# A chunk's norm in three queued steps, six gate products on GpSimd, and two drains less before the retention scan

## Chip, cores and metric

One core of one Trainium2 chip. The metric is the device time of one launch in microseconds (us), the median of several runs of the kernel.

## What is computed

A stream of 512 latent tokens and 256 context tokens, D = 1024, passes two layers. Layer 0 has a bidirectional mLSTM mixer (8 heads, keys of 64, values of 128), layer 1 a bidirectional retention mixer (8 heads, keys and values of 128). After each mixer stands a mixture of 16 experts with expert choice. All is float32. Of the first mixer's scan, per head and direction:

```python
s = einsum('bhid,bhjd->bhij', qc, kc) * exp(dmat - m_row[..., None])
num = einsum('bhij,bhjv->bhiv', s, vc) + w_inter[..., None] * einsum('bhid,bhdv->bhiv', qc, C)
den = s.sum(-1) + w_inter * einsum('bhid,bhd->bhi', qc, n)
h = num / maximum(abs(den), exp(-m_row))[..., None]
C_new = wc[..., None, None] * C + einsum('bhj,bhjd,bhjv->bhdv', wk, kc, vc)
```

The two directions are added, each head's 128 values are normed by their root mean square, multiplied by the norm's gain and by the sigmoid of an output projection, and projected back. The retention mixer is the same without the normaliser, with a fixed decay per head.

## The kernel before

Projections run in three matmul passes: weights and activations are each split into a high and a low part (`whi`, `wlo`, `hT_hi`, `hT_lo`), and `mm3` (L312 to L314) adds hi x hi, hi x lo and lo x hi in one PSUM tile `acc`. A pass of `Proj.run` takes 512 columns: for each token tile and each of 8 slices `k` it issues one triple of matmuls on 128x512. `split_piece` makes the parts, `whi` on ScalarE (L318) and `wlo` on VectorE (L319).

Beside the passes run generators. `bg` is a list of them; after every triple, `bg.step()` moves each on by one part, and a yielded number delays it by so many steps. `bg.drain()` runs all to their end at once. This sets the order in which instructions are handed to a scheduler, which orders each engine's queue from there. `tc.issue_after` queues what stands in it behind a given instruction. Nearly all transfers are issued by SyncE's queue, in order.

The first mixer's scan is worked in two blocks of four heads. `scan0(blk)` (L670) goes over six chunks of 128 tokens. `load` fetches qk, V, the rows E and the weights qw; `load_states` fetches the states Cz; `prep` (L706) masks E by GpSimd's affine_select (L711), takes eight exponentials on ScalarE (L715) and multiplies qw on VectorE (L717); `scores` (L720) makes S by matmul (L725) and A = S x E on VectorE (L731), four of them; `outputs` (L733) makes the numerators `num` (L739 with the states, L742 with A), the denominators `dn` and their reciprocal `rd`, and `yo` (L755 on ScalarE for one direction, L757 on VectorE for the other). `normed` (L760) takes the square on ScalarE (L762), a sum on VectorE (L764), a scale (L765), the power -1/2 on GpSimd (L766), and a product on VectorE (L767). `states` (L605) makes the states of the next block: `kw` on GpSimd (L612), `cu` by matmul (L618), C on VectorE (L622, L624), written by SyncE to DRAM (L628) for `load_states`.

The output projection is the pass that runs beside block 1's states and scan and beside the rest of block 0. Its end of a tile is `o_done` (L633): sigmoid on ScalarE (L636), times the gain `ng` on GpSimd (L637), times the normed chunk on VectorE (L638), write to DRAM (L639). There are six tiles per block, twelve in all.

In the retention mixer, `done` turns each projected q and k tile by rope (`qr`, `Kt`, the last step on GpSimd, L1694); `spill_T` (L1701) transposes it on TensorE (`tT`, L1705) and writes it to DRAM. `scan(blk)` (L1767) builds decay tables, then takes four chunks: it loads q, k, V and two states, makes scores `Sp`, `Ar`, `qs` and outputs `ro` (L1817), and norms them. Block 1's scan runs beside the pass of the gate.

Of the kernel before, what the change touches and what calls it, by code (L numbers as in the profile page):

```python
# [9 lines left out]
F32 = mybir.dt.float32  # L10
# [4 lines left out]
OP = mybir.AluOpType  # L15
# [5 lines left out]
T_LAT = 512  # L21
# [24 lines left out]
def backbone(ctx, tc, x, c, ctx_in, c_ctx, ada_w, ada_b, norm_mix_g, norm_ffn_g, final_norm_g,  # L46
# [460 lines left out]
    def mlstm_mixer(R):  # L507
# [125 lines left out]
        def o_done(blk, ng):  # L633
            def f(tt, p):
                e = pc.tile([128, 512], F32, name="oe", bufs=2)
                nc.scalar.activation(e, p, AF.Sigmoid)  # L636
                nc.gpsimd.tensor_tensor(e, e, ng, op=OP.mult)  # L637
                nc.vector.tensor_tensor(e, e, Y[blk, tt].rearrange("p h v -> p (h v)"), op=OP.mult)  # L638
                nc.sync.dma_start(y_d[0][tt][:, blk * 512:(blk + 1) * 512], e)  # L639
                gated.append(tt)  # L640
            return f
# [28 lines left out]
    def scan0(blk, sb, sp, pc, cols, flo, Y, gated):  # L670
# [35 lines left out]
        def prep(cc):  # L706
            t = L[cc]
            for d in range(2):
# [7 lines left out]
                if cc in prev0[d]:  # L716
                    nc.vector.scalar_tensor_tensor(t["qw"][:, d], t["qk"][:, 0:2], 0.125, t["qw"][:, d],  # L717
                                                   op0=OP.mult, op1=OP.mult)

        def scores(cc):  # L720
# [6 lines left out]
            for d in range(2):  # L727
                A = t["A", d] = sb.tile([128, 2, 2, 128], F32, name=f"A{d}")
                Ev = t["E"][:, d].rearrange("p (g q) i -> p q g i", q=2)
                for q in range(2):  # L730
                    nc.vector.scalar_tensor_tensor(A[:, q], S[q], 0.125, Ev[:, q], op0=OP.mult, op1=OP.mult)  # L731

# [26 lines left out]

        def normed(cc, y):  # L760
            j = sb.tile([128, 4, 128], F32, name="ysq", bufs=1)
            nc.scalar.activation(j, y, AF.Square)  # L762
            ss, rs = st("yss"), st("yrs")
            nc.vector.tensor_reduce(ss[:, 0:4], j, axis=mybir.AxisListType.X, op=OP.add)  # L764
            nc.vector.tensor_scalar(ss[:, 0:4], ss[:, 0:4], 1.0 / 128, EPS, op0=OP.mult, op1=OP.add)  # L765
            nc.gpsimd.tensor_tensor(rs[:, 0:4], ss[:, 0:4], neghalf[:, 0:4], op=OP.pow)  # L766
            nc.vector.tensor_tensor(y, y, rs[:, 0:4, None].to_broadcast([128, 4, 128]), op=OP.mult)  # L767
        load(order0[0])
# [6 lines left out]
        scores(order0[0])  # L775
        yield 1
        for n, cc in enumerate(order0):
            if n + 2 < len(order0):
                load(order0[n + 2])
            if n + 1 < len(order0):  # L780
                prep(order0[n + 1])
                yield 3
                scores(order0[n + 1])
                yield 4
            while len(gated) < 6 * blk + n - 5:
                yield 1
            y = pc.tile([128, 4, 128], F32, name="yo", bufs=6)
            outputs(cc, 0, y)
            yield 1
            outputs(cc, 1, y)  # L790
            normed(cc, y)
            Y[blk, cc] = y
            if n + 2 < len(order0):
                load_states(order0[n + 2])
            yield 2

    def gates(P, pp, tt_, wgp, gb, cols, flo, wcb, colp):
# [866 lines left out]
    def retention_mixer(R):  # L1664
# [33 lines left out]
        def ada_sums():  # L1698
            return [tmp[0].tile([128, 1024], F32, name="adasum", tag=f"y{i}", bufs=1) for i in (1, 2)]

        def spill_T(src, dst, tt):  # L1701
            yield 6
# [4 lines left out]
            nc.scalar.activation(t, p, AF.Copy)  # L1707
            nc.sync.dma_start(dram_ap(dst, (tt - 2) * 128, [[T_LAT, 128], [128 * T_LAT, 4], [1, 128]]), t)

        def done(what, blk):  # L1710
# [56 lines left out]
        def scan(blk):  # L1767

            sb = tmp[0]
            qd = [sb.tile([128, 4, 128], F32, name=f"qd{d}", bufs=1) for d in range(2)]  # L1770
            Dm = sb.tile([128, 4, 128], F32, name="Dm", bufs=1)
# [20 lines left out]
            yield 1  # L1792
            for cc in order1:
                tsl = [[T_LAT, 128], [128 * T_LAT, 4], [1, 128]]
                q = sb.tile([128, 4, 128], F32, name="qT", bufs=1)
                nc.sync.dma_start(q, dram_ap(qT_d[blk], (cc - 2) * 128, tsl))
                k = sb.tile([128, 4, 128], F32, name="kT", bufs=1)
                nc.sync.dma_start(k, dram_ap(kT_d[blk], (cc - 2) * 128, tsl))
                V = sb.tile([128, 4, 128], F32, name="Vr", bufs=1)
                nc.sync.dma_start(V.rearrange("p a b -> p (a b)"), Vr_d[blk][(cc - 2) * 128:(cc - 1) * 128, :])  # L1800
                S = []
                for d in range(2):
                    S.append(sb.tile([128, 4, 128], F32, name=f"Sl{d}", bufs=1))
                    nc.sync.dma_start(S[d].rearrange("p a b -> p (a b)"), S_d[blk][d, cc - 2])
                p = pp.tile([128, 4, 128], F32, name="Sp", tag="b", bufs=2)
# [42 lines left out]
        P.run(0, order1, done("q", 0), nxt=1536)  # L1848
        bg.drain()
        bg.add(scan(0), 0)  # L1850
# [4 lines left out]
        P.run(512, order1, done("q", 1), nxt=3072)  # L1855
        bg.drain()
        bg.add(scan(1), 2)
# [108 lines left out]
```

## Time and profile before

| | |
|---|---|
| three runs, us | 1913.15, 1916.28, 1919.35 |
| median, us | 1916.28 |
| the profiled execution, us | 1921.03 |
| its span, us | 1919.2 |
| mean granted clock of TensorE | 0.982 |
| busy share of the span: TensorE, VectorE, ScalarE, GpSimd | 95%, 38%, 22%, 15% |

The span is the time from the first to the last instruction; 1.8 us of the profiled execution lie around it. Times in the rows are us from the span's start unless marked ns. PE is TensorE's matmuls, DVE is VectorE, ACT ScalarE, POOL GpSimd, SP SyncE. A row names the line of the kernel, the engine, the operation and out<-in by the program's names. In a timeline, what stands in brackets is how long the engine stood idle before and what ended it. PEclk is the share of its full clock that TensorE was granted. Matmuls overlap, so two starts that follow each other tell the pace better than one's duration. The stages: the first mixer's scan and output lie at 240 to 480 us, the first mixture of experts up to 1060, the retention mixer up to about 1360, and the second mixture of experts behind.

### The profile page before, as it was taken

How to read it: one execution, taken by the hardware profiler on the slowest of the kernel's cores; microseconds unless marked ns; L12 is line 12 of the kernel's file. 1: busy time of each engine (PE TensorE's matmuls, PEld its weight loads, DVE VectorE, ACT ScalarE, POOL GpSimd, SP SyncE). 2: the span in 40 equal slices, each digit the busy share in tenths (PEclk: the TensorE clock that was granted, in tenths of full speed). 3: DMA queues.
4: the chain of work that ended last, by engine and by line, in shares of the span. 5: the costliest groups of instructions: out<-in, count | busy, mean ns of one | idle time of the engine just before them, and what ended most of it. 6: DMA issues, size and time to landing. Idle time of an engine off the chain costs nothing. (4 is left out here: it accounts for less than half of the span.)

```text
span 1919.2 us, 27783 instructions
## 1 busy us (share of the span) xinstructions
PE 1814.5 (95%) x11093; PEld 1029.8 (54%) x11093; DVE 730.0 (38%) x1742; ACT 429.1 (22%) x839; POOL 285.3 (15%) x343
## 2 busy tenths in 40 slices
PE   6999988999899999999999999999979999999997
PEld 2765676788444434444444777788764333333332
DVE  3554557646311111111113678454571322222224
ACT  3623356342200000000003621332421010100001
POOL 1110124201121111111001224334200000000001
PEclk9999999999899999999999999999998999999999
DMA  8568777672899999999996588445738999999996
GB/s 273 209 210 273 261 190 206 197 270 84 303 368 391 383 388 398 377 401 379 407 412 234 194 291 274 130 153 188 285 154 306 421 421 420 421 421 421 421 420 247
DMA packets 168578, 585.42 MB, mean 305 GB/s; under 512 B 16674, under 2 KB 68578, under 8 KB 114690
## 3 DMA queue, kind: packets, MB, share of 16 engines
q1 hardware_dynamic: 160176, 570.72, 78.3%
q0 software_dynamic: 6912, 12.71, 3.1%
q8 instruction: 88, 1.44, 0.3%
q10 hardware_dynamic: 1362, 0.23, 0.1%
q14 instruction: 40, 0.33, 0.0%
HBM read 544.13 MB, written 39.47 MB: 304 GB/s over the span
## 5 line engine op out<-in xcount | busy, mean ns | idle before, releaser
L1327 PE MATMUL y<-wslot,hT 128*32 128x256 f32 (+1 forms) x2016 | 278.7, 488 | 8.6 <-ACT hT L1493 8.4
L1327 PE MATMUL gl<-wslot,xs 128*64 128x512 f32 x1024 | 236.2, 605 | 7.1 <-DMA wslot<-in_moe_w_gate_dram 6.1
L1327 PE MATMUL ul<-wslot,xs 128*64 128x512 f32 x1024 | 229.9, 595 | 1.9 <-DMA wslot<-in_moe_w_up_dram 1.9
L312 PE MATMUL acc<-whi,hT_hi 128*128 128x512 f32 x544 | 223.3, 412 | 4.4 <-ACT hT_hi L382 3.1
L313 PE MATMUL acc<-wlo,hT_hi 128*128 128x512 f32 x544 | 218.0, 401 | 0.0
L314 PE MATMUL acc<-whi,hT_lo 128*128 128x512 f32 x544 | 217.3, 399 | 0.2 <-DVE hT_lo L383 0.2
L1327 PEld LDWEIGHTS y<-wslot,hT 128*32 128x32 f32 (+1 forms) x2016 | 100.0, 123 | 171.4 <-issue 131.8
L1476 DVE TENSOR_TENSOR hid<-hid,ul 128x512 f32<-128x512 f32 x32 | 22.0, 688 | 372.5 <-PE ul L1327 372.5
L1327 PEld LDWEIGHTS gl<-wslot,xs 128*64 128x64 f32 x1024 | 71.8, 138 | 155.5 <-issue 134.3
L1327 PEld LDWEIGHTS ul<-wslot,xs 128*64 128x64 f32 x1024 | 71.7, 137 | 148.3 <-issue 136.5
L312 PEld LDWEIGHTS acc<-whi,hT_hi 128*128 128x128 f32 x544 | 102.8, 189 | 39.2 <-issue 9.9
L314 PEld LDWEIGHTS acc<-whi,hT_lo 128*128 128x128 f32 x544 | 103.0, 189 | 28.5 <-issue 4.9
L313 PEld LDWEIGHTS acc<-wlo,hT_hi 128*128 128x128 f32 x544 | 103.4, 190 | 23.4 <-issue 2.8
L1473 ACT ACTIVATE hid<-gl 128x512 f32<-128x512 f32 x32 | 19.1, 598 | 414.9 <-PE gl L1327 414.9
L319 DVE TENSOR_TENSOR wlo<-wslot,whi 128x512 fp32r<-128x512 f32 x108 | 80.1, 758 | 55.8 <-ACT whi L318 55.3
L318 ACT ACTIVATE whi<-wslot 128x512 fp32r<-128x512 f32 x112 | 69.5, 630 | 107.3 <-PE acc L314 101.2
L1507 DVE SCALAR_TENSOR_TENSOR o<-y,gcol,M 128x512 f32<-128x512 f32 (+1 forms) x32 | 19.8, 617 | 143.8 <-PE y L1327 143.8
L1435 POOL TENSOR_TENSOR wslot<-x,wslot 128x512 f32<-128x512 f32 x4 | 5.0, 1277 | 443.3 <-DVE x L1378 443.3
L313 PE MATMUL po<-wol,yh 128*128 128x512 f32 x160 | 65.1, 407 | 2.0 <-DVE wol L319 1.9
L312 PE MATMUL po<-woh,yh 128*128 128x512 f32 x160 | 64.9, 407 | 1.0 <-ACT yh L952 0.8
L314 PE MATMUL po<-woh,yl 128*128 128x512 f32 x160 | 64.3, 403 | 0.0
L1493 ACT ACTIVATE hT<-hp 128x512 f32<-128x512 f32 (+1 forms) x48 | 24.6, 526 | 173.2 <-PE hp L1488 167.5
(450 smaller groups left out, 2517.4 us busy)
## 6 DMA issues: line engine op xcount, KB each, us to landing
wslot<-in_moe_w_up_dram SPq DMA_DIRECT2D x128, 1024.0 KB
wslot<-in_moe_w_gate_dram SPq DMA_DIRECT2D x128, 1024.0 KB
wslot<-in_moe_w_down_dram SPq DMA_DIRECT2D x124, 1024.0 KB
wslot<-in_ada_w_dram SPq DMA_DIRECT2D x40, 1024.0 KB
wslot<-in_ret_w_in_dram SPq DMA_DIRECT2D x16, 1024.0 KB
wslot<-in_mlstm_w_in_dram SPq DMA_DIRECT2D x12, 1024.0 KB
wslot<-in_ada_w_dram SPq DMA_DIRECT2D x16, 512.0 KB
E<-rows_d SPq DMA_DIRECT2D x24, 256.0 KB
```

Of the source, the lines that this page charges most:

```text
L312: nc.tensor.matmul(o, lh, rh, start=first, stop=False)
L313: nc.tensor.matmul(o, lh, rl, start=False, stop=False)
L314: nc.tensor.matmul(o, ll, rh, start=False, stop=last)
L318: nc.scalar.activation(wh, w, AF.Copy)
L319: eng.tensor_tensor(wl, w, wh.bitcast(F32), op=OP.subtract)
L1327: mm = nc.tensor.matmul(o[cw * q:cw * q + cw, :], stat(k), w(k)[:, qn * n:(qn + 1) * n], start=(k == 0), stop=(k == 7), tile_position=(0, ...
L1435: nc.gpsimd.tensor_tensor(O[:, lo], R.X[t][:, lo], fg[:, lo], op=OP.mult)
L1473: nc.scalar.activation(blocks_of(HID[v]), paired(o), AF.Silu)
L1476: nc.vector.tensor_tensor(h, h, paired(o), op=OP.mult)
L1493: LATE["act"] = nc.scalar.activation(HT[v], HP[v], AF.Copy)
L1507: LATE["dve"] = nc.vector.scalar_tensor_tensor(r, o, TOP[v][2][:, e:e + 1], M5[v], op0=OP.mult, op1=OP.mult)
```

## The change

The norm of a chunk becomes a generator of three steps: the square; the sum, scale and power; the product. The sum is queued behind the last qw product of the chunk two ahead, and the product behind its last A. `scan0` moves it on after `prep` and after `scores` of the next chunk that it works on, and ends it before the next norm. In `o_done`, the product with the normed chunk is on GpSimd for block 0. In the retention mixer, `scan` loads its first chunk before its tables, waits (while it is being ordered) until that chunk's q and k have been spilled, loads V and the states ahead of k and q, and is added without the two drains.

```diff
-                nc.vector.tensor_tensor(e, e, Y[blk, tt].rearrange("p h v -> p (h v)"), op=OP.mult)
+                (nc.vector if blk else nc.gpsimd).tensor_tensor(e, e, Y[blk, tt].rearrange("p h v -> p (h v)"), op=OP.mult)
...
-                    nc.vector.scalar_tensor_tensor(t["qw"][:, d], t["qk"][:, 0:2], 0.125, t["qw"][:, d],
+                    t["prep"] = nc.vector.scalar_tensor_tensor(t["qw"][:, d], t["qk"][:, 0:2], 0.125, t["qw"][:, d],
...
-                    nc.vector.scalar_tensor_tensor(A[:, q], S[q], 0.125, Ev[:, q], op0=OP.mult, op1=OP.mult)
+                    t["last"] = nc.vector.scalar_tensor_tensor(A[:, q], S[q], 0.125, Ev[:, q], op0=OP.mult, op1=OP.mult)
...
-        def normed(cc, y):
+        def normed(y, before, after):
             j = sb.tile([128, 4, 128], F32, name="ysq", bufs=1)
             nc.scalar.activation(j, y, AF.Square)
+            yield
             ss, rs = st("yss"), st("yrs")
-            nc.vector.tensor_reduce(ss[:, 0:4], j, axis=mybir.AxisListType.X, op=OP.add)
+            with behind_of(before):
+                nc.vector.tensor_reduce(ss[:, 0:4], j, axis=mybir.AxisListType.X, op=OP.add)
             nc.vector.tensor_scalar(ss[:, 0:4], ss[:, 0:4], 1.0 / 128, EPS, op0=OP.mult, op1=OP.add)
             nc.gpsimd.tensor_tensor(rs[:, 0:4], ss[:, 0:4], neghalf[:, 0:4], op=OP.pow)
-            nc.vector.tensor_tensor(y, y, rs[:, 0:4, None].to_broadcast([128, 4, 128]), op=OP.mult)
+            yield
+            with behind_of(after):
+                nc.vector.tensor_tensor(y, y, rs[:, 0:4, None].to_broadcast([128, 4, 128]), op=OP.mult)
+            yield
+
+        def behind_of(f):
+            ins = f()
+            return tc.issue_after(ins.ins) if ins is not None else contextlib.nullcontext()
...
                 prep(order0[n + 1])
+                next(open_, None)
                 yield 3
                 scores(order0[n + 1])
+                next(open_, None)
                 yield 4
...
             outputs(cc, 1, y)
-            normed(cc, y)
+            for _ in open_:
+                pass
+            nx2 = order0[n + 2] if n + 2 < len(order0) else None
+            open_ = normed(y, lambda c=nx2: L[c].get("prep") if c is not None else None,
+                           lambda c=nx2: L[c].get("last") if c is not None else None)
+            next(open_)
...
+            spilled.append((id(dst), tt))
...
+            def load(cc):
+                while not {(id(qT_d[blk]), cc), (id(kT_d[blk]), cc)} <= set(spilled):
+                    yield 1
...
+            q, k, V, S = yield from load(order1[0])
...
+            for n, cc in enumerate(order1):
+                if n:
+                    q, k, V, S = yield from load(cc)
+                    yield 1
...
         P.run(0, order1, done("q", 0), nxt=1536)
-        bg.drain()
         bg.add(scan(0), 0)
...
         P.run(512, order1, done("q", 1), nxt=3072)
-        bg.drain()
         bg.add(scan(1), 2)
```

What it does to the queues is seen at three places. The changed file's line numbers are one higher up to L759, four to six higher in the norm (sum L768, power L770, product L773), and 21 to 24 higher in the retention mixer.

VectorE, block 0 of the first mixer, from the end of the second chunk's outputs: before, then now.

```order
L764 TENSOR_REDUCE yss<-ysq 128x4
L765 TENSOR_SCALAR yss<-yss 128x4
L748 SCALAR_TENSOR_TENSOR dn<-num_2086,flo 128x2
L767 TENSOR_TENSOR yo<-yo,yrs 128x512
L750 TENSOR_TENSOR dn<-num_2086,dn 128x2
L751 RECIPROCAL rd<-dn 128x2
L748 SCALAR_TENSOR_TENSOR dn<-num_2087,flo 128x2
L731 SCALAR_TENSOR_TENSOR A_2056<-S_2050,E 128x256
L717 SCALAR_TENSOR_TENSOR qw<-qk,qw 128x256
L731 SCALAR_TENSOR_TENSOR A_2056<-S_2051,E 128x256
L731 SCALAR_TENSOR_TENSOR A_2059<-S_2050,E 128x256
L717 SCALAR_TENSOR_TENSOR qw<-qk,qw 128x256
```

```order
L732 SCALAR_TENSOR_TENSOR A_2055<-S_2049,E 128x256
L718 SCALAR_TENSOR_TENSOR qw<-qk,qw 128x256
L732 SCALAR_TENSOR_TENSOR A_2055<-S_2050,E 128x256
L732 SCALAR_TENSOR_TENSOR A_2058<-S_2049,E 128x256
L718 SCALAR_TENSOR_TENSOR qw<-qk,qw 128x256
L768 TENSOR_REDUCE yss<-ysq 128x4
L732 SCALAR_TENSOR_TENSOR A_2058<-S_2050,E 128x256
L769 TENSOR_SCALAR yss<-yss 128x4
L749 SCALAR_TENSOR_TENSOR dn<-num_2086,flo 128x2
L773 TENSOR_TENSOR yo<-yo,yrs 128x512
L751 TENSOR_TENSOR dn<-num_2086,dn 128x2
```

The first chunk's sum stood ahead of the third chunk's four A, with its scale and product; it now stands ahead of the last A, and its product behind it.

GpSimd at the boundary of the two blocks, from the third state product on (`kw` L612, mask L711, gain product L637, power L766; now L613, L712, L638, L770, and the gate product on L639): before, then now.

```order
L637 TENSOR_TENSOR oe_2863<-oe_2863,ng_2546 128x512
L711 AFFINE_SELECT E_2771<-E_2771 128x512
L612 TENSOR_TENSOR kw_2591<-knat_764,cols_166 128x256
L612 TENSOR_TENSOR kw_2608<-knat_764,cols_166 128x256
L711 AFFINE_SELECT E_2827<-E_2827 128x512 x2
L612 TENSOR_TENSOR kw_2625<-knat_764,cols_166 128x256
L612 TENSOR_TENSOR kw_2642<-knat_764,cols_166 128x256
L766 TENSOR_TENSOR yrs_2541<-yss_2540,neghalf_67 128x4
L637 TENSOR_TENSOR oe_2883<-oe_2883,ng_2546 128x512
L612 TENSOR_TENSOR kw_2659<-knat_764,cols_166 128x256
```

```order
L613 TENSOR_TENSOR kw_2591<-knat_764,cols_166 128x256
L712 AFFINE_SELECT E_2771<-E_2771 128x512
L613 TENSOR_TENSOR kw_2608<-knat_764,cols_166 128x256
L712 AFFINE_SELECT E_2771<-E_2771 128x512
L638 TENSOR_TENSOR oe_2863<-oe_2863,ng_2546 128x512
L770 TENSOR_TENSOR yrs_2533<-yss_2532,neghalf_67 128x4
L639 TENSOR_TENSOR oe_2863<-oe_2863,yo_2248 128x512
L613 TENSOR_TENSOR kw_2625<-knat_764,cols_166 128x256
L613 TENSOR_TENSOR kw_2642<-knat_764,cols_166 128x256
L613 TENSOR_TENSOR kw_2659<-knat_764,cols_166 128x256
```

Before, a mask or two stood between two pairs of `kw`; now a mask, a gain product, a power and a gate product stand between `kw_2608` and `kw_2625`.

TensorE in the retention mixer's gate pass of block 1, up to the last two transposes of q (`qr_10393`, `qr_10404`): before, then now. Before, the first row is in the third triple of the pass; now in the fifth.

```order
L312 MATMUL acc_10441<-whi_10279,hT_hi_8273 128x512
L313 MATMUL acc_10441<-wlo_10280,hT_hi_8273 128x512
L314 MATMUL acc_10441<-whi_10279,hT_lo_8274 128x512
L1705 MATMUL tT_10414<-ident_65,qr_10393 128x128 x4
L312 MATMUL acc_10445<-whi_10279,hT_hi_8273 128x512
L313 MATMUL acc_10445<-wlo_10280,hT_hi_8273 128x512
L314 MATMUL acc_10445<-whi_10279,hT_lo_8274 128x512
L312 MATMUL acc_10441<-whi_10310,hT_hi_8273 128x512
L313 MATMUL acc_10441<-wlo_10311,hT_hi_8273 128x512
L314 MATMUL acc_10441<-whi_10310,hT_lo_8274 128x512
L1705 MATMUL tT_10422<-ident_65,qr_10404 128x128 x4
```

```order
L313 MATMUL acc_10425<-whi_10310,hT_hi_8273 128x512
L314 MATMUL acc_10425<-wlo_10311,hT_hi_8273 128x512
L315 MATMUL acc_10425<-whi_10310,hT_lo_8274 128x512
L313 MATMUL acc_10429<-whi_10310,hT_hi_8273 128x512
L314 MATMUL acc_10429<-wlo_10311,hT_hi_8273 128x512
L315 MATMUL acc_10429<-whi_10310,hT_lo_8274 128x512
L1728 MATMUL tT_10491<-ident_65,qr_10393 128x128 x4
L313 MATMUL acc_10425<-whi_10328,hT_hi_8273 128x512
L314 MATMUL acc_10425<-wlo_10329,hT_hi_8273 128x512
L315 MATMUL acc_10425<-whi_10328,hT_lo_8274 128x512
L1728 MATMUL tT_10502<-ident_65,qr_10404 128x128 x4
```

The two transposes stood behind three and five triples of the pass; they now stand behind six and seven.

## Rows read from the trace of the kernel before

**Rows 1.** Busy time of each engine by stage: window, us, engines in us (x instructions), PEclk, DMA, GB/s.
```profile
240.00:400.00 160.00, 142.62 (x778) 113.78 (x778) 103.55 (x344) 84.14 (x199) 51.52 (x61) 0.94 0.70 205
400.00:480.00 80.00, 78.85 (x425) 65.77 (x424) 47.26 (x151) 25.15 (x54) 6.62 (x13) 1.00 0.43 158
480.00:1060.00 580.00, 566.34 (x4984) 248.50 (x4983) 98.98 (x264) 56.81 (x117) 84.24 (x86) 0.99 0.98 370
```

**Rows 2.** TensorE's waits, 240 to 400 us: line, what ended them, us in total, times, longest.
```profile
PE S L725 <- DVE A L731: 2.8, 1, 2.8
PE S L725 <- DVE dn L750: 2.5, 1, 2.5
PE num L739 <- DVE A L731: 2.3, 1, 2.3
PE cu L618 <- DVE C L624: 1.9, 1, 1.9
PE num L739 <- DMA Cz<-C_d: 1.2, 2, 0.7
PE acc L312 <- ACT oe L636: 1.2, 2, 0.8
...
PE num L739 <- ACT yo L755: 0.6, 1, 0.6
```

**Rows 3.** Timeline at 259 to 263 us: start, us, engine, line, [idle before <- releaser].
```profile
259.70 0.39 PE L313 MATMUL acc<-wlo,hT_hi 128*128 128x512 f32 x1
...
260.63 0.40 PE L314 MATMUL acc<-whi,hT_lo 128*128 128x512 f32 x1
...
260.89 1.14 DVE L767 TENSOR_TENSOR yo<-yo,yrs 128x512 f32<-128x512 f32 x1 [2.69 <-POOL yrs L766]
...
262.27 0.42 DVE L731 SCALAR_TENSOR_TENSOR A<-S,E 128x256 f32<-128x256 f32 x1
...
259.80 1.05 POOL L766 TENSOR_TENSOR yrs<-yss,neghalf 128x4 f32<-128x4 f32 x1
260.85 0.63 POOL L711 TENSOR_SCALAR_AFFINE_SELECT E<-E 128x512 f32<-128x512 f32 x1
```

**Rows 4.** Timeline of VectorE at 298 to 354 us: the norm's multiplications.
```profile
298.94 1.11 DVE L767 TENSOR_TENSOR yo<-yo,yrs 128x512 f32<-128x512 f32 x1 [0.80 <-POOL yrs L766]
...
309.67 1.76 DVE L767 TENSOR_TENSOR yo<-yo,yrs 128x512 f32<-128x512 f32 x1 [1.88 <-POOL yrs L766]
...
353.26 0.69 DVE L767 TENSOR_TENSOR yo<-yo,yrs 128x512 f32<-128x512 f32 x1 [0.80 <-POOL yrs L766]
```

**Rows 5.** Stretches of 10 us, columns as in the first group.
```profile
260.00:270.00 10.00, 6.78 (x28) 4.66 (x27) 7.95 (x26) 8.86 (x21) 5.70 (x7) 0.78 0.75 194
270.00:280.00 10.00, 10.00 (x56) 8.56 (x55) 6.39 (x24) 4.25 (x14) 1.89 (x3) 0.88 0.65 187
310.00:320.00 10.00, 8.12 (x55) 5.29 (x54) 7.83 (x19) 4.98 (x12) 4.13 (x5) 0.83 0.53 177
350.00:360.00 10.00, 7.25 (x32) 6.05 (x31) 7.89 (x30) 7.27 (x22) 2.91 (x4) 0.72 0.96 257
```

**Rows 6.** GpSimd's costliest groups, 240 to 400 us: xcount | busy us, mean ns | idle before.
```profile
L637 POOL TENSOR_TENSOR oe<-oe,ng 128x512 f32<-128x512 f32 x12 | 15.6, 1315 | 18.3 <-ACT oe L636 18.3
```

**Rows 7.** Timeline of VectorE at 266 to 333 us: two gate products.
```profile
266.69 1.65 DVE L638 TENSOR_TENSOR oe<-oe,yo 128x512 f32<-128x512 f32 x1
...
332.68 0.67 DVE L638 TENSOR_TENSOR oe<-oe,yo 128x512 f32<-128x512 f32 x1
```

**Rows 8.** GpSimd's waits, 240 to 400 us.
```profile
POOL E L711 <- DMA E<-rows_d: 60.8, 17, 12.7
```

**Rows 9.** Timeline of TensorE at 1202 to 1297 us, second mixer.
```profile
1202.02 0.46 PE L1817 MATMUL ro<-Vr,Ar 128*128 128x128 f32 x2 [2.51 <-DMA Vr<-Vr_d]
...
1294.31 0.66 PE L1705 MATMUL tT<-ident,qr 128*128 128x128 f32 x4 [1.79 <-POOL qr L1694]
...
1296.97 0.65 PE L1705 MATMUL tT<-ident,qr 128*128 128x128 f32 x4 [0.61 <-POOL qr L1694]
```

More of the change, by code (lines that the diff above doesn't have):

```diff
@@ L1 @@
+import contextlib
 import math
@@ L716, in prep @@
                 if cc in prev0[d]:
-                    nc.vector.scalar_tensor_tensor(t["qw"][:, d], t["qk"][:, 0:2], 0.125, t["qw"][:, d],
-                                                   op0=OP.mult, op1=OP.mult)
+                    t["prep"] = nc.vector.scalar_tensor_tensor(t["qw"][:, d], t["qk"][:, 0:2], 0.125, t["qw"][:, d],
+                                                               op0=OP.mult, op1=OP.mult)
         def scores(cc):
@@ L776, in scan0 @@
         yield 1
+        open_ = iter(())
         for n, cc in enumerate(order0):
@@ L795, in scan0 @@
             yield 2
+        for _ in open_:
+            pass
     def gates(P, pp, tt_, wgp, gb, cols, flo, wcb, colp):
@@ L1699, in ada_sums @@
             return [tmp[0].tile([128, 1024], F32, name="adasum", tag=f"y{i}", bufs=1) for i in (1, 2)]
+        spilled = []
         def spill_T(src, dst, tt):
@@ L1769, in scan @@
             sb = tmp[0]
+            tsl = [[T_LAT, 128], [128 * T_LAT, 4], [1, 128]]
+            def load(cc):
+                while not {(id(qT_d[blk]), cc), (id(kT_d[blk]), cc)} <= set(spilled):
+                    yield 1
+                V = sb.tile([128, 4, 128], F32, name="Vr", bufs=1)
+                nc.sync.dma_start(V.rearrange("p a b -> p (a b)"), Vr_d[blk][(cc - 2) * 128:(cc - 1) * 128, :])
+                S = []
+                for d in range(2):
+                    S.append(sb.tile([128, 4, 128], F32, name=f"Sl{d}", bufs=1))
+                    nc.sync.dma_start(S[d].rearrange("p a b -> p (a b)"), S_d[blk][d, cc - 2])
+                k = sb.tile([128, 4, 128], F32, name="kT", bufs=1)
+                nc.sync.dma_start(k, dram_ap(kT_d[blk], (cc - 2) * 128, tsl))
+                q = sb.tile([128, 4, 128], F32, name="qT", bufs=1)
+                nc.sync.dma_start(q, dram_ap(qT_d[blk], (cc - 2) * 128, tsl))
+                return q, k, V, S
+            q, k, V, S = yield from load(order1[0])
             qd = [sb.tile([128, 4, 128], F32, name=f"qd{d}", bufs=1) for d in range(2)]
@@ L1792, in scan @@
             yield 1
[L1793 to L1804, printed above, removed]
+            for n, cc in enumerate(order1):
+                if n:
+                    q, k, V, S = yield from load(cc)
+                    yield 1
                 p = pp.tile([128, 4, 128], F32, name="Sp", tag="b", bufs=2)
```

## Prediction, made before the change was run

> **What bounds the kernel now.** I read the busy time of each engine by stage first. In the first mixer's scan, 240 to 400 us, TensorE is busy 142.62 of 160 us, so 17.4 us are open there; between 400 and 480 it is busy 78.85 of 80 us, and in the first mixture of experts 566.34 of 580 us with the DMA engines at 0.98 [rows 1]. The change touches the two mixers only, and there TensorE ends last, so a change is worth the idle time of TensorE that it closes or opens. What a mixer gains is kept: the stream of expert weights that bounds the next stage starts when the mixer gives its buffers free, and between 400 and 480 us the DMA engines are only 0.43 busy [rows 1], so an earlier end starts the stream earlier by as much. I take the same for the second mixer.
>
> Second, TensorE's waits in that window, by what ended them [rows 2]. Three of the four long ones stand on VectorE: scores that wait for the score products A or for `dn` behind them (2.8 and 2.5 us), and numerators that wait for A (2.3); the fourth is the state product `cu`, which waits for the update of C (1.9).
>
> Third, the order of time around the first of these [rows 3]. The norm's last multiplication starts at 260.89 after 2.69 us in which VectorE stood still for GpSimd's power; A, queued behind it, starts at 262.27. On GpSimd the power (1.05 us) stands between the two masks of one E tile. The block boundary and the chunk after it show the same [rows 4]: the multiplication at 298.94 waited 0.80 us and took 1.11; that at 309.67 waited 1.88 and took 1.76, with C's updates behind it; that at 353.26 waited 0.80 and took 0.69.
>
> Fourth, the granted clock by 10 us [rows 5]: a share under 1 means that part of the stretch ran at 1.2 instead of 2.4 GHz. After the gaps of 2.3 us at 261, 1.9 at 310 and 2.8 at 352 the stretches show 0.78 and 0.88, 0.83, and 0.72. The clock that is missing is 10 x (0.22 + 0.12) = 3.4 us, 1.7 and 2.8. The gap of 2.5 at 298 has no such row.
>
> **The change, part by part.** The sum is made against the profiled execution, 1921.03 us, which is 4.75 above the median of the three runs, 1916.28; the difference is carried to the median as it is.
>
> *Third chunk of block 0.* The norm's reduction and multiplication go behind the next chunk's A. The two masks of E then follow each other, so the second is done 1.05 us sooner, and A need not wait for the multiplication (1.14) [rows 3]; TensorE also gets four projection matmuls ahead of the numerators. Its two gaps there are 2.3 and 0.8, the longer wait for the sigmoid `oe` [rows 2], 3.1 in all. What is late next is E: its exponentials start when the mask does, and the mask waits for a load. So I take half, **-1.5** (bounds 0 and -3.1).
>
> *Small waits.* The other wait for `oe` (0.4), the longer of the two for Cz (0.7) and a numerator's for ScalarE's `yo` (0.6) make 1.7 [rows 2]. Projection matmuls, which now lie in more pieces between the numerators, cover most of it: **-1.2** (bounds 0 and -1.7).
>
> *Block boundary.* The waits of 2.5 and 1.9 us, 4.4 together, stand behind one multiplication each that had waited for its power [rows 2, 4]. Both may go. But on GpSimd the new order puts a mask, a norm-gain product, a power and a gate product between `kw_2608` and `kw_2625`: 0.63 + 1.3 + 1.05 + 1.3 = 4.3 us [rows 3, 6], while TensorE has 0.6 us of work between the two `cu` that read them (a `cu` and one projection matmul). That opens a wait of 3.7. One multiplication still stands ahead of C's updates, as that at 309.67 did: 1.9 again. SyncE's queue has the write of the first gated tile ahead of the second write of C, and so ahead of the loads of Cz; it hangs on the same GpSimd product and ends no later. -4.4 + 3.7 + 1.9 = **+1.2** (bounds -4.4, and +9.2: no old wait goes, the 3.7 comes, and two multiplications hold C for a power and themselves, 2 x (1.05 + 1.76) = 5.6).
>
> *Block 1, at 352.* The wait of 2.8 us at 352 [rows 2] ended with an A that stood behind the multiplication at 353.26, 0.80 + 0.69 = 1.5 us with its wait [rows 4]. That goes; the loads are as late as before, so the rest stays: **-1.4** (bounds 0 and -2.8).
>
> *Clock.* With the gaps at 261 and 352 cut to half, one of the two falls goes, 3.4 or 2.8 [rows 5]; at the boundary the longer gap may bring half a fall more, 0.9. -3.4 + 0.9 = **-2.5** (bounds -7.9, all three gone, and +1.7, one more as at 310).
>
> *Gate product.* Six of twelve go to GpSimd. Its product of this size takes 1.3 us [rows 6], on VectorE 0.67 alone [rows 7]: 6 x 1.3 = 7.8 us come onto an engine that is busy 51.52 of 160 us [rows 1] and stood 60.8 us for loads of E [rows 8], and at least 6 x 0.67 = 4.0 leave VectorE. That idle time is the cover; where a product stands ahead of a mask or `kw` it is gone, and the boundary has that price. Another cost: the VectorE product at 266.69, beside a GpSimd product, took 1.65 in place of 0.67 [rows 7], so each of the six can hold up VectorE by 1.0. Bounds 0 and +6.0; most of VectorE's work is waited for by no one, so **+0.5**.
>
> The Trainium skill (GPSIMD Engine Reference, sections 4.1 Engine selection and 8 Key points) speaks against this part: an elementwise operation on a tile belongs on VectorE, GpSimd being about half as fast with two inputs, and since the two share their interfaces to SBUF, they contend where VectorE reads two inputs. This trace agrees on the first (1.3 against 0.67) and shows the second at 266.69. By that rule the term would be the upper bound, +6.0, and the predicted time 5.5 us longer.
>
> *Second mixer.* Two drains ahead of the retention scan go. In block 0 the transposes of q keep their places and the first chunk's loads theirs in SyncE's queue: nothing moves. In block 1 the last two transposes of q, for which TensorE stood 1.79 and 0.61 us [rows 9], go from behind three and five triples of matmuls of the next pass to behind six and seven. A matmul is issued every 0.23 us (259.70 to 260.63 are four steps [rows 3]), so three triples are 2.1 us and cover the first wait; of both, 2.4, I take **-2.1** (bounds 0 and -2.4). The gap of 2.5 us before `ro`, which waits for Vr [rows 9], has that load ahead of two others now, but a weight load of 1 MB two places earlier, too: **-0.7**, one triple's worth (bounds -2.5 and +0.7, the same the other way).
>
> **Sum:** -1.5 - 1.2 + 1.2 - 1.4 - 2.5 + 0.5 - 2.1 - 0.7 = -7.7; from the median, **1908.6 us**. A measurement of this kernel can tell about 0.3%, 5.7 us, from no change.
>
> **Rivals.** *No change to be seen.* GpSimd's masks stood 60.8 us for loads of E, up to 12.7 at a time [rows 8]. If E is what A waits for once the multiplication is out of its way, A comes no earlier, and the gaps at 261, 310 and 352 keep their length and their clock. Only the small waits and the transposes count then: -1.2 - 2.1 = -3.3, 1913.0. For it: the second mask at 260.85 came late itself. Against it: VectorE stood 2.69 us for the power [rows 3] while A was queued behind. A weaker form lies in my forecast: the second mixer's part moves nothing, -7.7 + 2.8 = -4.9, 1911.4.
>
> *Slower.* At the block boundary all goes through GpSimd: `cu` waits for `kw`, `kw` for gate products, C for `cu` and the multiplications, Cz for C. At its upper bound that is 9.2; with one more fall of the clock, 1.7, and VectorE held up by 1.0 beside each of the four GpSimd products there, it is 14.9. The other terms without the clock give -6.9. Sum +8.0, 1924.3. The kernel is slower from where the boundary costs 6.9, and by over 0.3% from 12.6. For it: two products and a power between two `kw`, and 0.6 us of matmuls to cover them. Against it: later in that stretch eight projection matmuls stand between the last two `cu`, and VectorE's old wait of 1.88 for a power [rows 4] was already counted at the same place.
>
> That the change doesn't do what it says is settled by the new order: the norm, the product and block 1's transposes do move, the rest of the second mixer's part does not.
>
> **How the numbers follow.** My forecast 0.58, of which 0.07 is its weaker form; the first rival 0.25; the second 0.17. Faster by over 0.3%: 0.58 - 0.07 = 0.51; within 0.3%: 0.25 + 0.07 = 0.32; slower: 0.17. The range begins at 1899: half of what is left to their lower bounds for the chunks at 261 and 352 (-0.8, -0.7) and boundary (-2.8), the clock without its falls at 261 and 352 (-2.8), the rest of Vr's wait and the small waits (-2.3), in all -9.4. It ends at 1922, which takes in the first rival and the milder half of the second.
>
> **What would show it.** Right: TensorE's waits for A near 261 and 352 under 1.5 us and a full clock after one of them; VectorE's wait for the power nearly gone; no wait of tT for qr in block 1; the new wait of `cu` for `kw` near 3.7. Wrong: A that waits for E through ScalarE; waits of `cu` or `num` of over 5 us in all at the boundary; a lower clock than 0.83 there; VectorE's two-input operations near 1.7 more often than before. The prediction falls if TensorE's busy share in the scan, 142.62 of 160, hardly grows.

## The result, and the profile after the change

The changed kernel is **slower**: 1933.25 us, median of 7 runs (1924.99 to 1935.95), beside 1920.35 for the kernel before (7 runs, 1913.15 to 1924.58). The ratio is 1.0066, 95% interval 1.0047 to 1.0085. The forecast was 1908.6, faster, and the range ended at 1922. It was counted from the median of three runs, 1916.28; from the median of seven the same -7.7 would give about 1912.7.

First, where the time lies. The window below runs in each kernel from the first score matmul of the scan (L725, now L726) to the first matmul behind the first mixer (`pr`, L1112, now L1133). Columns are as in [rows 1]. The kernel before:

```profile
240.00:474.40 234.40, 215.91 (x1169) 175.06 (x1168) 147.52 (x485) 106.33 (x245) 54.52 (x69) 0.96 0.61 191
```

And the changed kernel:

```profile
238.20:484.00 245.80, 220.21 (x1170) 177.96 (x1169) 146.50 (x479) 105.53 (x245) 63.70 (x75) 0.92 0.61 183
```

The first mixer takes 245.8 us in place of 234.4, 11.4 more; its scan began 1.8 us sooner in this execution, so it ends 9.6 us later. From there to the end of the span it is 1444.8 before and 1447.3 after, so most of the loss is in this window. It has two parts. TensorE's idle time there grew from 234.40 - 215.91 = 18.5 us to 25.6, by 7.1; and its busy time grew from 215.9 to 220.2, by 4.3, for the same matmuls (the records are 1169 and 1170), while the granted clock fell from 0.96 to 0.92.

The waits of TensorE between 240 and 400 us, in the form of [rows 2]:

```profile
PE acc L313 <- ACT oe L637: 7.0, 3, 4.1
PE num L740 <- ACT yo L756: 5.9, 3, 5.3
PE cu L619 <- DVE C L623: 3.8, 1, 3.8
PE S L726 <- DMA qk<-qk_d: 2.1, 3, 1.2
PE num L743 <- ACT yo L756: 1.7, 2, 1.3
```

The waits for A that the change was to take away are gone. In their place stand a projection that waits for the sigmoid (4.1 at the longest), a numerator that waits for ScalarE's `yo` (5.3) and a `cu` that waits for C (3.8). The clock around and behind them, as in [rows 5]; the second line lies at two shorter waits, of 1.15 us at 282.83 and 1.28 at 285.35:

```profile
260.00:270.00 10.00, 7.24 (x25) 5.66 (x26) 8.42 (x29) 7.32 (x17) 6.56 (x6) 0.54 0.73 186
280.00:290.00 10.00, 7.57 (x34) 6.14 (x33) 7.72 (x29) 5.86 (x18) 2.27 (x3) 0.74 0.81 220
310.00:320.00 10.00, 9.99 (x54) 6.57 (x55) 4.81 (x16) 0.09 (x1) 3.37 (x6) 0.56 0.63 196
340.00:350.00 10.00, 4.66 (x19) 3.64 (x18) 6.23 (x23) 4.17 (x12) 7.23 (x6) 0.81 0.75 209
```

Three timelines show the three places. The first stands at 261 to 266 us:

```profile
260.99 0.68 DVE L768 TENSOR_REDUCE yss<-ysq 128x4 f32<-128x512 f32 x1
...
261.58 0.41 DVE L732 SCALAR_TENSOR_TENSOR A<-S,E 128x256 f32<-128x256 f32 x1
...
261.91 0.16 DVE L769 TENSOR_SCALAR yss<-yss 128x4 f32<-128x4 f32 x1
...
262.16 1.05 POOL L770 TENSOR_TENSOR yrs<-yss,neghalf 128x4 f32<-128x4 f32 x1 [2.96 <-DVE dn L749]
...
262.46 0.80 PE L313 MATMUL acc<-whi,hT_hi 128*128 128x512 f32 x1 [4.14 <-ACT oe L637]
...
263.24 1.77 DVE L773 TENSOR_TENSOR yo<-yo,yrs 128x512 f32<-128x512 f32 x1 [1.11 <-POOL yrs L770]
...
265.99 1.23 PE L740 MATMUL num<-Cz,qw 128*128 128x258 f32 x2 [0.29 <-ACT yo L756]
```

The sum of the norm (260.99) stands one A ahead of the product's place, so the power begins at 262.16 and the product again waits 1.11 us for it, then takes 1.77. The multiplications of [rows 3, 4] waited 2.69, 0.80, 1.88 and 0.80 for theirs. On TensorE the projection matmul at 262.46 has waited 4.14 us for the sigmoid, and the numerators, whose A were done by 261.99, stand behind it till 265.99. The last 0.29 us of that they wait for `yo`, whose `dn` stood behind the product.

The second is the block boundary, at 303 to 311 us:

```profile
305.64 1.28 POOL L638 TENSOR_TENSOR oe<-oe,ng 128x512 f32<-128x512 f32 x1
...
306.87 1.01 POOL L770 TENSOR_TENSOR yrs<-yss,neghalf 128x4 f32<-128x4 f32 x1
307.85 1.26 POOL L639 TENSOR_TENSOR oe<-oe,yo 128x512 f32<-128x512 f32 x1
307.91 1.75 DVE L773 TENSOR_TENSOR yo<-yo,yrs 128x512 f32<-128x512 f32 x1 [3.71 <-POOL yrs L770]
...
309.14 0.33 SPq L640 DMA_DIRECT2D y<-oe  x1
...
309.58 0.28 DVE L623 COPY C<-cu 128x129 f32<-128x129 f32 x1
...
310.01 1.13 PE L619 MATMUL cu<-V,kw 128*64 128x129 f32 x8 [3.83 <-DVE C L623]
```

Gain product, power and gate product follow each other on GpSimd as its new order has them. VectorE's product waits 3.71 us for the power, the last copy of C stands behind it, and `cu` waits 3.83 for that copy. SyncE issues the gated tile's write only at 309.14; it had been idle since 304.4, with C's next writes queued behind.

The third is at 338 to 348 us:

```profile
338.40 1.51 POOL L638 TENSOR_TENSOR oe<-oe,ng 128x512 f32<-128x512 f32 x1 [4.87 <-ACT oe L637]
...
343.44 1.26 POOL L639 TENSOR_TENSOR oe<-oe,yo 128x512 f32<-128x512 f32 x1
...
344.67 1.01 POOL L770 TENSOR_TENSOR yrs<-yss,neghalf 128x4 f32<-128x4 f32 x1
...
345.63 1.67 POOL L712 TENSOR_SCALAR_AFFINE_SELECT E<-E 128x512 f32<-128x512 f32 x2
345.70 1.11 DVE L773 TENSOR_TENSOR yo<-yo,yrs 128x512 f32<-128x512 f32 x1 [3.47 <-POOL yrs L770]
346.30 0.40 ACT L716 ACTIVATE E<-E,cols 128x128 f32<-128x128 f32 x1 [5.17 <-POOL E L712]
346.74 0.15 DVE L749 SCALAR_TENSOR_TENSOR dn<-num,flo 128x2 f32<-128x2 f32 x1
...
347.37 1.14 ACT L756 ACTIVATE yo<-num,rd 128x128 f32<-128x128 f32 x4 [0.67 <-DVE dn L749]
...
348.05 1.23 PE L740 MATMUL num<-Cz,qw 128*128 128x258 f32 x2 [5.34 <-ACT yo L756]
```

Four GpSimd products, two gain and two gate products from 338.40 to 344.7, stand ahead of a power. VectorE's product waits 3.47 us for it, the next chunk's `dn` (346.74) stands behind that product, ScalarE's `yo` (347.37) waits for `dn`, and the numerator, whose buffer `yo` frees, waits 5.34. A second chain runs beside this one and is nearly as long: the two masks (345.63) stand behind the same four products and the power, and an exponential that waits 5.17 us for the first of them stands ahead of `yo` in ScalarE's queue. It ends at 346.70, so `dn` alone made `yo` later by 0.67 us.

In the second mixer, TensorE's waits of tT for qr fell and that of `ro` for Vr fell from 2.5 to 0.7, with a new one for qT. The waits for qr before, and then three rows of now:

```profile
PE tT L1705 <- POOL qr L1694: 3.6, 4, 1.8
```

```profile
PE tT L1728 <- POOL qr L1715: 2.4, 3, 1.3
...
PE Sp L1841 <- DMA qT<-qT_d: 1.1, 1, 1.1
PE ro L1851 <- DMA Vr<-Vr_d: 0.7, 1, 0.7
```

From the first transposition of K there to the end of the span it is 853.75 us before and 855.56 after.

### The profile page after: what moved, and what is told of

Same layout as the page of the kernel before. It is cut to its first block, busy times and chain, and to the rows that moved or that the text cites. A ratio compares the mean times of both kernels' runs of the same rounds, so it can differ in the third digit from the quotient of the medians.

```text
span 1931.3 us, 27807 instructions
## 1 busy us (share of the span) xinstructions
PE 1820.0 (94%) x11093; PEld 1034.2 (54%) x11093; DVE 731.6 (38%) x1736; ACT 428.1 (22%) x839; POOL 294.8 (15%) x349
## 5 line engine op out<-in xcount | busy, mean ns | idle before, releaser
L314 PEld LDWEIGHTS acc<-wlo,hT_hi 128*128 128x128 f32 x544 | 103.9, 191 | 22.5 <-issue 2.2
```

The costliest lines, as they stand in the source:

```text
L314: nc.tensor.matmul(o, lh, rl, start=False, stop=False)
```

## The experiments

All ratios are against the kernel before, from runs on the same chip.

**One part alone.** Two theories were put: that the gate products on GpSimd are the loss (G), or the split norm (N).

`e1_gate_back`, the changed kernel with

```diff
-                (nc.vector if blk else nc.gpsimd).tensor_tensor(e, e, Y[blk, tt].rearrange("p h v -> p (h v)"), op=OP.mult)
+                nc.vector.tensor_tensor(e, e, Y[blk, tt].rearrange("p h v -> p (h v)"), op=OP.mult)
```

> The changed kernel with the six gate products back on VectorE; norm and second mixer as changed. Theory G (the loss comes from GpSimd: gate products stand ahead of powers and kw): the 5.3 us gap of num at 348 and about half of the 3.8 us gap of cu at 310 go, with the clock they cost; -8 to -12 us against the changed kernel, so a ratio to the kernel before of 0.996 to 1.002. Theory N (the loss comes from the norm's split, which puts projection matmuls ahead of numerators on TensorE, where they wait for the sigmoid): both the 4.1 us gap at 262 and most of the loss stay, ratio 1.004 to 1.007.

Measured: 1.0009 (0.9995 to 1.0023).

`e2_gate_alone`, the kernel before with that line the other way round:

> The kernel before with six gate products on GpSimd and nothing else. Theory G: slower by 5 to 9 us (ratio 1.003 to 1.005), with a new TensorE wait of 3 us or more near 340 to 350 that VectorE's wait for the power explains. Theory N: ratio 0.998 to 1.002, no new wait over 2 us.

Measured: 0.9997 (0.9983 to 1.0011).

`e3_norm_alone`, the kernel before with the hunks of the diff in `prep`, `scores`, `normed` and the loop of `scan0`:

> The kernel before with the norm in three steps and nothing else. Theory G: ratio 0.996 to 1.001. Theory N: ratio 1.003 to 1.007, with the gap of about 4 us at 262 (acc that waits for the sigmoid).

Measured: 1.0012 (0.9996 to 1.0027).

`e4_mixer2_alone`, the kernel before with the hunks in the retention mixer:

> The kernel before with the retention scan's loads and the two drains as changed and nothing else. Both theories: ratio 0.998 to 1.000 (about -2 us: the two waits of tT for qr in block 1 shrink from 2.4 to 1.3 us and the wait for Vr from 2.5 to 0.7, as in the changed kernel's trace, against a new one of 1.1 for qT).

Measured: 0.9997 (0.9984 to 1.0009).

None of the parts alone is the loss: by the intervals the split can be 0.27% of it at most (e3), the gate products 0.11% (e2). e1 alone would have spoken for G, but G falls with e2, as N does with e3. The gap that theory N named did come in e3, and longer than in the changed kernel:

```profile
262.98 0.50 PE L313 MATMUL acc<-whi,hT_hi 128*128 128x512 f32 x1 [4.40 <-ACT oe L637]
```

So this gap is the split's, and by itself it doesn't make the loss. In e3's profiled execution, 1926.01 us, the first mixer takes 237.3 us with 22.5 us of TensorE idle, so 2.9 and 4.0 more than before the change.

VectorE's wait for the power shows why the split alone brings nothing. In the changed kernel it reads, between 240 and 400 us:

```profile
DVE yo L773 <- POOL yrs L770: 19.4, 11, 3.7
```

In e2:

```profile
DVE yo L767 <- POOL yrs L766: 18.0, 12, 3.1
```

And in e3:

```profile
DVE yo L773 <- POOL yrs L770: 14.5, 11, 2.7
```

Before the change:

```profile
DVE yo L767 <- POOL yrs L766: 14.5, 12, 2.7
```

The split left the wait at 14.5; the gate products made it 18.0. In VectorE's queue the split changed what stands behind the waiting product: A before, `dn` and C now.

**Parts together.** `e5_norm_gate` has the norm's and the gate product's hunks, and `e9_gate_mixer2` the gate product's and the retention mixer's:

> The kernel before with the norm in three steps and the six gate products on GpSimd, second mixer as before. Theory I (the two parts cost only together, since with the norm's product put late each of its powers and products stands behind gate products): ratio 1.005 to 1.008, scan gaps at about 262 (4 us), 310 (4 us) and 348 (5 us), and more clock missing between 240 and 400 us than the 10 us of the kernel before. Theory M (the second mixer's part is needed for the loss): ratio 1.000 to 1.002.

Measured: 1.0058 (1.0039 to 1.0077), gaps of 4.35, 4.05 and 5.35 us at 266, 312 and 350 us, and 13.6 us of clock missing between 240 and 400 us.

> The kernel before with the six gate products on GpSimd and the second mixer's part, the norm as before. If the loss is the norm's split together with the gate products, this one has none: ratio 0.997 to 1.001, the first mixer's scan as long as before, and a gap of cu at the boundary of 2 us or less. If any two parts together cost, ratio 1.003 or more.

Measured: 0.9991 (0.9977 to 1.0006), a gap of `cu` of 1.07. So it is the norm and the gate product together, and no part of the second mixer's shows in these runs.

**The places.** `e6_last_two_back` and `e7_boundary_two_back` put two gate products each back on VectorE, the condition being the count of tiles done:

```diff
-                (nc.vector if blk else nc.gpsimd).tensor_tensor(...
+                (nc.vector if blk or len(gated) in (4, 5) else nc.gpsimd).tensor_tensor(...
...
+                (nc.vector if blk or len(gated) in (2, 3) else nc.gpsimd).tensor_tensor(...
```

> The changed kernel with the last two of block 0's six gate products back on VectorE. Theory I, with the place at 338 to 345 us (four GpSimd products in a row ahead of a power): the 5.3 us gap falls to 1.5 to 3, -3 to -6 us against the changed kernel, ratio 1.003 to 1.005. Theory B (the boundary at 310 decides): ratio stays 1.006 or more.

Measured: 1.0059 (1.0039 to 1.0079). The gap at 348 fell from 5.34 to 3.94, but others of 2.6 at 333 and 2.5 at 368 opened. Theory I's place falls: two products off the queue at 338 to 345 bring nothing that the ratio shows.

> The changed kernel with the third and fourth of the six gate products, those between the kw of the block boundary, back on VectorE. Theory B: the 3.8 us gap of cu falls to about 2.5 and the clock after it stays higher; -4 to -8 us against the changed kernel, ratio 1.002 to 1.005. Theory I at 338 to 345: ratio 1.005 or more.

Measured: 1.0039 (1.0023 to 1.0055); the gap of `cu` fell from 3.83 to 1.41 us, that at 348 to 3.50 at 344. By the ratios (1.0066 and 1.0039) the boundary, with what follows from it at 344, is some 0.3%, but the two intervals overlap.

`e8_three_E` gives E a third buffer (`name="E", bufs=3`):

> The changed kernel with three buffers for E in the first mixer's scan in place of two, so that its loads go out a chunk earlier. If the masks' wait for E's loads holds ScalarE's exponentials, and the sigmoid behind them, and so the projection that waits for the sigmoid, the gap of acc at 262 falls from 4.1 to under 2 us and GpSimd's wait for E from some 60 us to under 30: -3 to -6 us against the changed kernel, ratio 1.003 to 1.005. If E's loads are only late because nobody waits for them, the gap at 262 stays and the ratio is 1.006 or more.

Measured: 1.0078 (1.0055 to 1.0101); the gap at 262 is 4.27 and GpSimd's wait for E 57.7 us, beside 53.8 in the changed kernel. Buffers are not what makes E late. In this kernel's trace SyncE issues the third chunk's E at 252.39, behind four loads of qw and four of Cz, some 3 us for each four, and the mask that needs it runs at 257.86.

`e10_write_later` collects block 0's six writes of gated tiles:

```diff
-        Y, gated = {}, []
+        Y, gated, late = {}, [], []
...
-                e = pc.tile([128, 512], F32, name="oe", bufs=2)
+                e = pc.tile([128, 512], F32, name="oe", bufs=6)
...
-                nc.sync.dma_start(y_d[0][tt][:, blk * 512:(blk + 1) * 512], e)
+                late.append((y_d[0][tt][:, blk * 512:(blk + 1) * 512], e))
+                if blk or len(gated) == 5:
+                    for dst, src in late:
+                        nc.sync.dma_start(dst, src)
+                    late.clear()
```

> The changed kernel with block 0's six writes of gated tiles issued together at the end of that block (six buffers for oe in place of two), so that SyncE's queue does not stand for a gate product at the boundary, as it does in the changed kernel from 304.4 to 309.1; GpSimd's order at the boundary then has the gate product ahead of the third kw and not between a power and a kw. Theory S (SyncE's queue, or GpSimd's order that its write brings, is what makes the boundary costly): the gap of 3.8 us at 310 falls under 2.5, the later gap of 5.3 at 348 falls too, ratio 1.000 to 1.003. Theory L (three lengthened chains, of which none is SyncE's): ratio 1.005 or more.

Measured: 1.0047 (1.0029 to 1.0065). The waits of `cu` at the boundary are 1.27 and 1.00 us, so that place is mended, but the numerator's gap at 348 is 4.79. The ratio lies between those of the two theories and its interval reaches into both, so it decides for neither. The edit moved GpSimd's order as well, so what SyncE's own stand cost isn't told apart.

`e11_first_norm_whole` runs the first chunk's norm at once in block 0:

```diff
-            nx2 = order0[n + 2] if n + 2 < len(order0) else None
+            nx2 = order0[n + 2] if n + 2 < len(order0) and (blk or n) else None
...
             next(open_)
+            if blk == 0 and n == 0:
+                for _ in open_:
+                    pass
```

> The changed kernel with the norm of the first chunk of block 0 whole, as before, and all others in three steps. If the split makes TensorE wait at 262 for the sigmoid (projection matmuls put ahead of numerators), that gap of 4.1 goes back to the form of the kernel before, 2.3 for A and 0.8 for the sigmoid, -1 to -3 us against the changed kernel, ratio 1.004 to 1.006. If the gap at 262 is E's load in any order, it stays at 4 and the ratio at 1.006 or more.

Measured: 1.0044 (1.0028 to 1.0061), with the gap in its old form on TensorE's timeline:

```profile
265.53 0.70 PE L740 MATMUL num<-Cz,qw 128*128 128x258 f32 x2 [2.69 <-DVE A L732]
...
267.44 0.79 PE L313 MATMUL acc<-whi,hT_hi 128*128 128x512 f32 x1 [0.76 <-ACT oe L637]
```

So the split is what put the projection matmuls ahead of the numerators at 262. The gaps behind it changed too (2.65 us at the boundary, 4.69 at 344), so the ratio doesn't price that place alone.

**The link.** `e12_no_power` takes the power out of the first mixer's norm:

```diff
-            nc.gpsimd.tensor_tensor(rs[:, 0:4], ss[:, 0:4], neghalf[:, 0:4], op=OP.pow)
+            nc.vector.tensor_scalar(rs[:, 0:4], ss[:, 0:4], -0.5, None, op0=OP.mult)
```

> The changed kernel with the norm's power on GpSimd replaced by a scaling on VectorE, so that the chunks are scaled by a wrong factor (the power of the first mixer's norm is left out). The norm then hangs on no GpSimd instruction. Theory P (the gate products cost by standing ahead of the power, behind which VectorE's product, dn, the numerators' buffers and C wait): gaps at 310 and 348 below 2 us, ratio 0.998 to 1.002. Theory Q (they cost by kw and the masks of E behind them): the gap at 310 stays at 3 us or more, ratio 1.004 or more.

Measured: 0.9984 (0.9972 to 0.9996); the `cu` gap at the boundary is 3.38 us but stands behind ScalarE's `yo`, and the numerator's gap at 338 is 3.02. The ratio is P's, while both gaps stayed above 3. The timeline of the second:

```profile
336.83 0.40 ACT L716 ACTIVATE E<-E,cols 128x128 f32<-128x128 f32 x1 [4.16 <-POOL E L712]
...
337.14 1.12 ACT L756 ACTIVATE yo<-num,rd 128x128 f32<-128x128 f32 x4
...
337.80 0.70 PE L740 MATMUL num<-Cz,qw 128*128 128x258 f32 x2 [3.02 <-DMA y<-oe]
```

The profile puts it down to the write of a gated tile, but the numerator starts 0.66 us after `yo`, as in the changed kernel (0.68), and `yo` stands behind an exponential that waited 4.16 us for a mask. So at this place the masks behind the gate products, theory Q's, hold TensorE about 3 us even without a power, though with no loss in the ratio. The power wasn't the only thing that changed: VectorE has no wait for GpSimd in the norm at all, so this bounds what the norm's way through GpSimd costs and doesn't show which part of it does.

`e13_product_late` leaves every operation on its engine, and its edit moves only the norm's product: behind the last `yo` of the next chunk, not the last A of the chunk after it.

```diff
-                        nc.vector.scalar_tensor_tensor(y[:, i, :], num[j][:, q, 0:128], rd[:, q:q + 1], y[:, i, :],
+                        t["fin"] = nc.vector.scalar_tensor_tensor(y[:, i, :], num[j][:, q, 0:128], rd[:, q:q + 1], y[:, i, :],
...
                 scores(order0[n + 1])
-                next(open_, None)
...
+            nx1 = order0[n + 1] if n + 1 < len(order0) else None
...
-                           lambda c=nx2: L[c].get("last") if c is not None else None)
+                           lambda c=nx1: L[c].get("fin") if c is not None else None)
```

> The changed kernel with the norm's product queued behind the last yo of the next chunk, so behind that chunk's dn, in place of behind the last A of the chunk after it. Theory P with VectorE's order as the link at 348 (product waits for the power, dn stands behind the product, the numerators wait for their buffers): the gap of 5.3 us at 348 falls under 3, that at 262 (4.1) stays; ratio 1.002 to 1.005. If dn is not the link: ratio 1.006 or more, gap at 348 of 4 or more.

Measured: 1.0005 (0.9995 to 1.0015). Its first mixer's window:

```profile
238.60:472.70 234.10, 213.60 (x1169) 172.67 (x1169) 145.62 (x479) 106.16 (x245) 62.76 (x75) 0.96 0.63 192
```

VectorE's wait for the power, between 240 and 400 us:

```profile
DVE yo L773 <- POOL yrs L770: 4.6, 3, 2.6
```

The window is 234.1 us, as before the change; of the 11.7 us won back 5.1 are idle time of TensorE and 6.6 busy time. The clock is 0.96 again, and the wait for the power has fallen from 19.4 us to 4.6, with all six gate products still on GpSimd and in the boundary's old place, behind a mask, a gain product and a power. Where the gap of 348 was, the timeline of this kernel has:

```profile
327.86 0.96 POOL L712 TENSOR_SCALAR_AFFINE_SELECT E<-E 128x512 f32<-128x512 f32 x1 [12.04 <-DMA qw<-rows_d]
...
334.08 0.15 DVE L749 SCALAR_TENSOR_TENSOR dn<-num,flo 128x2 f32<-128x2 f32 x1
334.24 1.01 POOL L770 TENSOR_TENSOR yrs<-yss,neghalf 128x4 f32<-128x4 f32 x1
...
334.71 0.63 ACT L756 ACTIVATE yo<-num,rd 128x128 f32<-128x128 f32 x2 [3.66 <-DVE dn L749]
...
335.39 0.70 PE L740 MATMUL num<-Cz,qw 128*128 128x258 f32 x2 [3.11 <-ACT yo L756]
```

`dn` (334.08) no longer waits for the power (334.24). A numerator still waits 3.11 us there, where under 3 was expected, the gap at 262 stayed, at 3.57, and that of `cu` at the boundary is 2.41; the ratio came out lower than expected. Moving the norm's product back is thus worth nearly the whole loss. Other queues were reordered with it: here one mask (327.86) runs ahead of the four GpSimd products, and `yo` (334.71) stands ahead of the exponentials of the second. So at this place e13 doesn't tell `dn` from the mask.

`e16_three_mended` joins the edits of e13, e11 and e7 on the changed kernel:

> The changed kernel with three things mended at once: the first chunk's norm whole, the two gate products at the block boundary back on VectorE, the norm's product behind the next chunk's outputs. If the three places make up the loss: gaps of the scan together 20 us or less, no clock fall beyond the kernel before's, ratio 0.996 to 1.000, and perhaps faster than both kernels. If the split of the norm costs in itself: 1.001 to 1.003.

Measured: 1917.04 us against 1919.32, ratio 0.9984 (0.9970 to 0.9998). The first mixer's window:

```profile
240.00:469.00 229.00, 211.27 (x1169) 171.91 (x1169) 145.22 (x481) 105.95 (x245) 59.94 (x73) 0.97 0.63 196
```

The first mixer takes 229.0 us, 5.4 less than before the change, with 17.7 us of TensorE idle, where 20 or less was expected. This version is faster than both kernels, by 0.16% against the one before, a gain that the interval only just keeps apart from none.

## Why the prediction was wrong

**What bounds the kernel, and that a mixer's gain or loss is kept:** right. The first mixer ends 9.6 us later than before, and the span is 12.1 longer (1931.3 against 1919.2).

**Third chunk, -1.5: the step that failed, and the sign with it.** A did come sooner, and no matmul waits for it. But the step took the product out of A's way and forgot whose way it was put in. It also took the sum along: the sum stands one A ahead of the product, so the power (1.05) can't be done when the product's turn comes, and VectorE stands still as long as before, 14.5 us in e3 and, with gate products ahead of the power, 19.4 in the changed kernel. Behind the product there now stands `dn`, and behind `dn` the buffers that the numerators need. The prediction had asked what is queued behind the power and A, not what is behind the product's new place; with the product one place further back (e13) the ratio is 1.0005 in place of 1.0066. And the four projection matmuls ahead of the numerators, booked as filler, need a buffer that the sigmoid frees behind eight exponentials: the gap became 4.14 and 0.29 for 2.3 and 0.8. e11 shows that the split does this, and e3 (4.40) and e13 (3.57) that such a gap alone is not the loss.

**Small waits, -1.2:** not met. A wait for the sigmoid of 1.68 us, one for Cz of 0.80 and one for `yo` of 1.28 stand in the changed kernel, beside that of 1.15 for the sigmoid that is counted at the boundary.

**Block boundary, +1.2:** near in size, in part by luck. The old waits of 4.4 went, and the gaps of 0.77, 1.15 and 3.83 there make 5.75, +1.4. But the new wait was put at 3.7 for a `cu` behind `kw`, and no `cu` waited for `kw`: that of 310.01 starts when C's copy (309.58 to 309.86) is done. What came is the other term, the product ahead of C, put at 1.9 as before: the product's wait for the power grew from 1.88 to 3.71, since a mask, which waits for a load, and a gain product now stand ahead of that power. Wrong as well is that the write in SyncE's queue "ends no later": it went out at 309.14, where that of before went at 302.33.

**Block 1 at 352, -1.4:** the gap there went, and one of 5.34 opened at 348. The prediction charged gate products only where they stand ahead of `kw`; here they stand ahead of the power, and of the next chunk's masks. That was the second part of the failed step. e13 cuts the gap to 3.11 and takes the loss away; e12, without the power, leaves 3.02 behind a mask.

**Clock, -2.5:** wrong sign. Against 10.2 us of missing clock in the sixteen stretches of 10 us before there are 17.1 after. As longer busy time it is +4.3. The longest gap doesn't settle it: in e3 10.1 us are missing, as before the change, with a gap of 4.40.

**Gate product, +0.5:** right for the part alone (e2: 0.9997). The upper bound of +6.0, by which the prediction took the rule in GPSIMD Engine Reference (sections 4.1 Engine selection and 8 Key points) of the Trainium skill, wasn't met by it either. What the products cost depends on what stands behind the power that they delay (e5 and e13: 1.0058 and 1.0005 with the same six on GpSimd).

**Second mixer, -2.8:** not seen. The transposes' gap fell from 2.4 us to 1.3 and Vr's from 2.5 to 0.7, but new waits for qT (1.1), for a state (0.6) and for a buffer that ScalarE frees (0.7) came, and those for K's transposes grew by 0.6. The part alone gives 0.9997 (0.9984 to 1.0009), 0.6 us faster, with an interval that ends at 3.1.

**The rivals.** The slower one, 1924.3, had the right sign and the right engine; its 9.2 should be 9.3 (3.7 + 5.6). It saw the boundary as the place; e7 and e10, which mend it, give back about 0.2 to 0.3% of the 0.66%. Two of the prediction's signs of being wrong came there: `cu` and `num` waited over 5 us (0.80, 0.77 and 3.83), and the clock was 0.56, under 0.83. The one of no change, with E as the limit, had E's loads late in all kernels, but e8 shows that buffers don't move them and e13 that the loss doesn't hang on them.

What stays open: at 348, how much is `dn` behind the product and how much the masks behind the gate products, since no run holds ScalarE's order while it moves the product; and how the loss divides between the three places. e7, e10, e11 and e13 each mend one and give back 0.27, 0.19, 0.22 and 0.61%, more in sum than was lost; they are not independent, and the intervals of the first three overlap that of the changed kernel. As causes the runs show the pair of edits (e2, e3, e5) and the place of the norm's product (e13).

## What to carry to other kernels

To take a waiting instruction out of another's way, look at what stands behind its new place in the same queue, and follow it to the buffers that it frees. Split a chain so that each step has the length of the step before it as distance: a sum that moves with its product leaves the wait between them as long as it was (14.5 us here). Two edits that each cost nothing can cost much together when one lengthens a wait and the other puts the critical work behind that wait, so they are to be measured together.

## What was not expected of the hardware

The gaps' cost is more than their length: 7.1 us of added idle time came with 4.3 us of slower matmuls. In the changed kernel the matmuls are slow from the end of the gap of 4.14 on (a projection matmul took 0.80 us at 262.46, a pair of numerators 1.23 at 265.99). In the kernel before, a pair took 0.70 at 263.36, right behind the gap of 2.33, but 1.20 at 265.90. VectorE's product of the norm took 1.77 us at 263.24 and 1.11 at 345.70, beside GpSimd's work, where its shortest is 0.69 [rows 4]; and GpSimd is held up as well: its gain products take 1.3 us each [rows 6], but the two from 263.19 in the changed kernel took 2.94 together.
